# Residual rows added earlier in the last stage of a hybrid encoder, and a reordered start

## The chip, the cores and the metric

The kernel runs on one core of one Trainium2 chip. The metric is the device time of one execution in microseconds (us), taken as the median of several runs. One execution is also profiled, and the profile's span and instruction times come from that one.

## The reference, cut to what matters

One layer of a bidirectional encoder runs over two batches with shared weights: the prompt (512 rows of 1024) and the sample (1024 rows of 1024), all in fp32.

```python
def _trunk(x, ...):
    h = _rmsnorm(x, norm_attn_g)
    z = h @ w_in                                   # 1024 -> 1792: q, k, v, and the conv pair ca, cb
    a_out = _window_attn(q, k, v, bias, band, sink)  # window 128, T5 bias, a sink per head
    c = ca * sigmoid(cb)
    c = _dwconv(c, conv_dw_w, conv_dw_b)           # 31 taps
    c = silu(_layernorm(c, conv_ln_g, conv_ln_b))
    x = x + concat([a_out, c]) @ w_out
    h = _rmsnorm(x, norm_ffn_g)
    u = _dwconv(h @ w_up, ffn_dw_w, ffn_dw_b)      # 1024 -> 5632, 3 taps
    x = x + (silu(u[..., :D_FF]) * u[..., D_FF:]) @ w_down   # D_FF = 2816 -> 1024
    return _rmsnorm(x, norm_final_g)
```

Below, x1 is the value of x after the out-projection: the last residual sum adds it to the product with w_down.

## The kernel before, in words

**Products.** An fp32 operand is split into a high part, rounded to the fp32r format of TensorE, and a low part, the difference. A product is three matmuls: high by high, high by low, low by high (L1502, L1503, L1504; in the input projection all from L504). The high part is a cast on ScalarE, the low part a subtraction on VectorE or GpSimd (L1050 is the line of the helper `sub`, L1047 of the helper `add`). All matmuls that matter here are 128x128 by 128x512.

**Stages.** Input projection, attention and the 31-tap convolution, out-projection, the feed-forward part of the prompt, and last the up and the down product of the sample. These last two use a Strassen-Winograd scheme with 7 products in place of 8.

**The start.** A tile of weights in pieces (`w_first`, five DMAs from L214) and the eight blocks of the transposed prompt (`load_xT(0)`, L200) are loaded first. On ScalarE a tiny Exp (L220) draws in the table that the activations need. A few transposes of the identity (L224) run on TensorE meanwhile. For each weight piece in turn, `first_pieces` scales the x block (L459), casts the piece (L470) and takes its low half on GpSimd (L471); `beside` (L504) then issues six matmuls for each of the eight blocks. The sample's rows follow. They need the row scales, which come from the rows of x_prompt and end at L240.

**The down stage.** The products run in the order 1, 2, 5, 6, 7, 4, 3 (ORDER). Each is a sum over 11 pairs p (NPAIR) of blocks of the contracted axis. In a pair there are six row blocks tt with three matmuls each, so a product is 198 matmuls. The operands of pair p are loaded (`load_next`, from L1433 and L1440), summed or subtracted where the scheme wants it, and split (`operands`) four to six pairs ahead. A product fills three wide PSUM banks, two row blocks in each; there are four such banks, w in the profile. Two are taken at p = 0. The third, for tt = 4 and 5, is taken at p = HOLD, and the matmuls for the pairs before are then made up for. At the end of a product `evacuate` adds its banks to sums in SBUF, `u`, `e`, `o11` and `o12`, on VectorE; a bank is free for the next product after that. Product 3 has a loop of its own: z (tt 0, 1) from the start, zp (tt 4, 5) from p = HOLD, and at p = 4 two banks zs for the rest.

**The x1 rows.** `load_x1(t, n)` loads one quarter of x1 with six DMAs of 256 KB (L1514) into three tiles. `with_x(name, t, n)` adds it to one of the four sums: three adds of 128x1024, the first on VectorE and the other two on GpSimd.

**What sets the order.** Each engine works off its instructions in one order. In the last stages the order of TensorE and of the DMA issues on SyncE (SP) is that of the program. The order on ScalarE, VectorE and GpSimd is set when the kernel is built, by a scheduler that simulates the timeline.

Of the kernel before, what the change touches and what calls it, by code (L numbers as in the profile page):

```python
# [12 lines left out]
AF = mybir.ActivationFunctionType  # L13
ALU = mybir.AluOpType

P = 128
# [44 lines left out]
KL, WN = 16, 7  # L61
LN = 3
SUM_AT = (4, 6, 8, 10, 12, 14, 16, 18)
XP = (2, 4, 4, 8, 8, 10)
LZ = 6
AP = 1

# [37 lines left out]
def tile_hybrid_encoder(ctx: ExitStack, tc: tile.TileContext, xs, rel_bias, norm_attn_g, w_in,  # L105
                        attn_sink, conv_dw_w, conv_dw_b, conv_ln_g, conv_ln_b, w_out, norm_ffn_g,
                        w_up, ffn_dw_w, ffn_dw_b, w_down, norm_final_g, onehot, laid, outs):
    nc = tc.nc
# [8 lines left out]
    sb = Slots(lambda tag: sml if tag[0] == "s" else big,  # L117
               dict(q=(15, 4096), c=(4, 4352), h=(61, 2048), d=(2, 2304), s=(33, 64)))
# [12 lines left out]
    nhalf = cst.tile([P, 4], F32, name="nhalf")  # L131
    warm = cst.tile([P, 4], F32, name="warm")
# [63 lines left out]
    def load_xT(nt):  # L196
        n = 1 if nt == 0 else 2
        for k in range(0, KC, n):
            x = sb.tile([n, NT])
            nc.sync.dma_start(x[:], xT[nt][k:k + n].rearrange("k p t -> p k t"))  # L200
            for m in range(n):
                xq[nt, k + m] = (x, m)
            x = None

    def load_rows(nt):
        G, t0 = (GR[0], 0) if nt == 0 else (GR[1], 4 * (nt - 1))
        for tt in range(4):
            xq[nt, "row", tt] = load_x(G, t0 + tt)

    h1, xq, rbs, first_w = {}, {}, {}, []  # L210
    PIECES = ((0, 1), (1, 1), (2, 2), (4, 2), (6, 2))
    for k0, n in PIECES:
        w = sb.tile([n, 2 * P])
        nc.scalar.dma_start(w[:], laid["w_first"][k0:k0 + n].rearrange("k p c -> p k c"))  # L214
        first_w.append(w)
        w = None
    load_xT(0)
    load_rows(0)
    load_xT(1)
    nc.scalar.activation(warm[:], nhalf[:], AF.Exp)  # L220
    for _ in range(NW // 4):
        pt = bank("step")
        for i in range(4):
# [288 lines left out]
    cvw = cst.tile([P, 128], F32, name="cvw")  # L512
    fw = cst.tile([P, 192], F32, name="fw")
    nc.sync.dma_start(cvw[:, :CK * 4], laid["cvw"])
    load_xT(2)
    want_raw(2)
    nc.sync.dma_start(fw[:, :132], laid["fw"])
    nc.sync.dma_start(sinkb[:], attn_sink[0].partition_broadcast(P))
# [300 lines left out]
    def double_keys():  # L819
        for kv in range(NKV):  # L820
            for L in range(2):
                nc.gpsimd.tensor_copy(kt[1, kv][L][HD:P, :], kt[1, kv][L][0:HD, :].bitcast(F32))
                yield
# [69 lines left out]
    n, doubling = 0, double_keys()  # L893
# [152 lines left out]
    def add(out, a, b, eng=None):  # L1046
        (eng or nc.vector).tensor_tensor(out, a, b, op=ALU.add)  # L1047
# [176 lines left out]
    def wide():  # L1224
        return wide_banks.tile([W2])
# [7 lines left out]
    def armed(out, hi=None):  # L1233

        hi = hi or A[1, 0][0]
        nc.tensor.matmul(out, hi[:, 0:P], hi[:], start=True, stop=True)  # L1236
# [206 lines left out]
    ORDER = (1, 2, 5, 6, 7, 4, 3)  # L1443
# [48 lines left out]
    HOLD = 2  # L1492
# [16 lines left out]
    def load_x1(t, n):  # L1509
        xd[t, n] = pair2()  # L1510
        for w in range(3):
            for q in range(2):
                blk = 2 * t + q if w == 2 else 4 + 4 * t + 2 * w + q
                nc.sync.dma_start(xd[t, n][w][:, q * NT:(q + 1) * NT], x1d[blk][:, n * NT:(n + 1) * NT])  # L1514
# [26 lines left out]
    def with_x(name, t, n):  # L1541
        x = xd.pop((t, n))
        for w in range(3):
            add(acc[name][w][:], acc[name][w][:], x[w][:], nc.gpsimd if w else None)
# [55 lines left out]
    def down_step(k):  # L1600
        i, p = steps[k]
        if k > 1:
            next(rest, None)
        load_next(8 if k == 0 else 3 if len(pr) < CAP else 0)
        make(k + (LEAD + max(0, min(2, (k - 60) // 2)) if k else 1))
        if p == 0:
            pd.extend(wide() for _ in range(2))
        hold = 5 if i == ORDER[0] else HOLD
        if p == hold:
            pd.append(wide())  # L1610
        for tt in range(4):
            mm_down(pd[tt // 2][:, (tt % 2) * NT:(tt % 2 + 1) * NT], i, p, tt)
        hl[i, p] = None, hl[i, p][1]
        if p >= hold:
            for q in range(p + 1) if p == hold else (p,):
                for tt in (4, 5):
                    mm_down(pd[2][:, (tt % 2) * NT:(tt % 2 + 1) * NT], i, q, tt)
                hl.pop((i, q)), hp.pop((i, q))
        if i == 7 and p == 4:
            load_x1(0, 0)  # L1620
        if i == 7 and p == 8:
            with_x("o11", 0, 0)
        if i == 4 and p == XP[0]:
            load_x1(1, 1)
            fins.append(sb.tile([D]))
            nc.sync.dma_start(fins[0][:], norm_final_g.partition_broadcast(P))
            nc.scalar.activation(fins[0][:], fins[0][:], AF.Identity, scale=D ** 0.5)
        if i == 4 and p == XP[1]:
            with_x("e", 1, 1)
        if i == 4 and p == XP[2]:  # L1630
            load_x1(0, 1)
        if i == 4 and p == XP[3]:
            with_x("o12", 0, 1)
        if i == 4 and p == XP[4]:
            load_x1(1, 0)
        if i == 4 and p == XP[5]:
            with_x("u", 1, 0)
        if p == NPAIR - 1:
            evacuate(i, pd)
            while pd:  # L1640
                pd.pop(0)

    for j in range(2, NJ):
# [52 lines left out]
    for p in range(NPAIR):  # L1696
        load_next(LN)
        make(base + p + LZ)
        for tt in (0, 1):
            mm_down(z[:, tt * NT:(tt + 1) * NT], 3, p, tt)  # L1700
        if p == HOLD:
            zp = wide()
        if p >= HOLD:
            for q in range(p + 1) if p == HOLD else (p,):
                for tt in (4, 5):
                    mm_down(zp[:, (tt - 4) * NT:(tt - 3) * NT], 3, q, tt)
                hp.pop((3, q))
        if p == 4:
            for tt in (2, 3):
                zs.append(wide())  # L1710
                armed(zs[-1][:, L], hl[3, p][0][0])
                nc.scalar.copy(zs[-1][:, L], cut(o12, tt))
        if p in OTHER:
            blk = OTHER[p]
            tt = blk + 2 if blk < 4 else blk - 8
            finish(blk, (cut(u, tt), cut(e, tt)), False)
# [81 lines left out]
```

## Time and profile before

| | before |
|---|---|
| median of 3 runs | 1512.12 us (1510.12 to 1512.32) |
| the profiled execution | 1509.46 us |
| its span in the trace | 1507.7 us |
| granted TensorE clock, mean | 0.993 |
| last matmul begins | 1501.41 us |

A busy row of the profile gives each engine's busy time and its share of the span. A row of a timeline gives the start, the duration, the engine (a "q" behind it means that the engine issues a DMA), the line of the code, the operation with the tiles it writes and reads (buffer numbers left out), and in brackets the idle time before it with the instruction that ended it. Waits have the line that waited, what ended the wait, the total, the count and the longest. A row of windows gives, for one stretch of time, each engine's busy time with its count of instructions, then the granted TensorE clock (1.00 is full), the share of the DMA engines and their GB/s.

### The profile page before, as it was taken

To read this page: it belongs to the slowest core of one execution; us is meant where nothing else is said; L and a number is where in the kernel's file an instruction comes from. 1 tells how busy PE (TensorE), PEld (TensorE's weight loads), DVE (VectorE), ACT (ScalarE), POOL (GpSimd) and SP (SyncE) were. 2 spreads that over 40 slices of the span, in tenths; PEclk is the share of its full clock that TensorE was granted. 3 is DMA by queue.
4 is the path that set the end of the run, shared out by engine and by line. 5 is a ranking of instruction groups with operands and counts; after the bars stand their busy time and mean duration, and the time that the engine had idled before them with its cause. 6 is when DMAs were issued, how large, how long until landed. Compare 5 with 4: busy or idle time off the path is not lost. (4 is left out here: it accounts for less than half of the span.)

```text
span 1507.7 us, 19878 instructions
## 1 busy us (share of the span) xinstructions
PE 1478.4 (98%) x6736; PEld 1215.9 (81%) x6736; DVE 1115.0 (74%) x1512; ACT 801.8 (53%) x1421; POOL 779.7 (52%) x687
## 2 busy tenths in 40 slices
PE   8999999999999999999999999999999999999988
PEld 7888778777888888878788788888888888888776
DVE  7877945648999895566769888888886756657883
ACT  6424455567777876653464545454454453433354
POOL 3455253356987864332436666555654341214756
PEclk9999999999999999999999999999999999999999
DMA  9465241743433453763114334433323493446843
GB/s 377 154 173 143 89 112 36 243 145 129 154 122 127 144 170 130 226 208 105 70 59 137 133 133 133 133 126 126 130 102 111 163 339 124 132 151 208 270 134 153
DMA packets 124625, 228.19 MB, mean 151 GB/s; under 512 B 20419, under 2 KB 45763, under 8 KB 124396
## 3 DMA queue, kind: packets, MB, share of 16 engines
q1 hardware_dynamic: 122988, 225.32, 45.6%
q10 hardware_dynamic: 1536, 1.61, 0.3%
q8 instruction: 53, 0.87, 0.2%
q14 instruction: 48, 0.39, 0.1%
HBM read 166.83 MB, written 61.10 MB: 151 GB/s over the span
## 5 line engine op out<-in xcount | busy, mean ns | idle before, releaser
L159 POOL TENSOR_TENSOR q<-q,q 128x1024 fp32r<-128x1024 f32 x66 | 158.6, 2405 | 78.4 <-ACT q L158 47.1
L1050 POOL TENSOR_TENSOR q<-q,q 128x512 fp32r<-128x512 f32 x81 | 116.4, 1445 | 128.6 <-ACT q L1156 128.6
L1502 PE MATMUL w<-h,h 128*128 128x512 f32 x436 | 170.8, 392 | 5.7 <-DVE q L1047 5.7
L1050 DVE TENSOR_TENSOR h<-h,h 128x512 fp32r<-128x512 f32 (+1 forms) x153 | 127.0, 856 | 66.1 <-ACT h L1058 24.1
L1504 PE MATMUL w<-h,h 128*128 128x512 f32 x432 | 168.8, 391 | 0.0
L1503 PE MATMUL w<-h,h 128*128 128x512 f32 x426 | 166.7, 391 | 0.0
L293 PE MATMUL u<-h,q 128*128 128x512 f32 x384 | 151.0, 394 | 0.0
L295 PE MATMUL u<-h,q 128*128 128x512 f32 x384 | 150.4, 392 | 0.0
L294 PE MATMUL u<-h,q 128*128 128x512 f32 x384 | 150.1, 391 | 0.0
L1170 PE MATMUL w<-h,q 128*128 128x512 f32 x368 | 143.8, 391 | 0.9 <-ACT w L1261 0.6
L1172 PE MATMUL w<-h,q 128*128 128x512 f32 x368 | 143.7, 391 | 0.0
L1171 PE MATMUL w<-h,q 128*128 128x512 f32 x347 | 135.4, 390 | 0.0
L1050 POOL TENSOR_TENSOR h<-h,h 128x512 fp32r<-128x512 f32 (+1 forms) x38 | 56.3, 1484 | 148.6 <-ACT h L1485 112.9
L1058 ACT CAST h<-h 128x512 fp32r<-128x512 f32 x116 | 69.7, 620 | 104.2 <-DVE h L1050 38.4
L1502 PEld LDWEIGHTS w<-h,h 128*128 128x128 f32 x436 | 82.4, 189 | 23.7 <-DVE q L1047 6.5
L330 DVE SCALAR_TENSOR_TENSOR c<-d,cvw,c 128x512 f32<-128x512 f32 x128 | 95.9, 749 | 1.7
L158 ACT CAST q<-q 128x1024 fp32r<-128x1024 f32 x66 | 69.1, 1050 | 50.8 <-PE u L294 25.0
L1504 PEld LDWEIGHTS w<-h,h 128*128 128x128 f32 x432 | 81.7, 189 | 17.1
L1050 POOL TENSOR_TENSOR c<-q,c 128x512 fp32r<-128x512 f32 x46 | 73.1, 1598 | 40.6 <-ACT c L1156 40.5
L1503 PEld LDWEIGHTS w<-h,h 128*128 128x128 f32 x426 | 80.5, 189 | 16.8
L322 POOL TENSOR_TENSOR h<-h,h 128x512 f32<-128x512 f32 x62 | 80.5, 1301 | 18.5 <-ACT h L321 16.3
L295 PEld LDWEIGHTS u<-h,q 128*128 128x128 f32 x384 | 72.1, 188 | 14.7
(459 smaller groups left out, 4017.2 us busy)
## 6 DMA issues: line engine op xcount, KB each, us to landing
q<-in_laid_w_up SPq DMA_DIRECT2D x88, 512.0 KB, 4.0
ga<-q SPq DMA_DIRECT2D x65, 256.0 KB, 2.2
h<-gap SPq DMA_DIRECT2D x57, 256.0 KB, 3.6
h<-ga SPq DMA_DIRECT2D x57, 256.0 KB, 3.1
h<-in_w_down SPq DMA_DIRECT2D x52, 256.0 KB, 3.4
q<-in_laid_w_in SPq DMA_DIRECT2D x22, 512.0 KB, 4.0
gap<-h SPq DMA_DIRECT2D x44, 256.0 KB, 3.0
q<-in_x_sample SPq DMA_DIRECT2D x15, 512.0 KB, 7.2
```

Of the source, the lines that this page charges most:

```text
L159: (nc.vector if dve else nc.gpsimd).tensor_tensor(lo[:], raw[:], hi[:].bitcast(F32), op=ALU.subtract)
L293: nc.tensor.matmul(out, whi[:, kc, :], hi[:], start=(kc == 0), stop=False)
L294: nc.tensor.matmul(out, whi[:, kc, :], lo[:], start=False, stop=False)
L295: nc.tensor.matmul(out, wlo[:, kc, :], hi[:], start=False, stop=(kc == KC - 1))
L330: nc.vector.scalar_tensor_tensor(acc[:], src(t), w(t), acc[:], op0=ALU.mult, op1=ALU.add)
L1050: (eng or nc.vector).tensor_tensor(out, a, b, op=ALU.subtract)
L1170: nc.tensor.matmul(out, whi[:, s], hi[:], start=(start and c == 0), stop=False, **go)
L1171: nc.tensor.matmul(out, whi[:, s], lo[:], start=False, stop=False, **go)
L1172: nc.tensor.matmul(out, wlo[:, s], hi[:], start=False, stop=(stop and c == 3), **go)
L1502: nc.tensor.matmul(out, sh[:, c], th[:], start=(p == 0 and not seeded), stop=False, **go)
L1503: nc.tensor.matmul(out, sh[:, c], tl[:], start=False, stop=False, **go)
L1504: nc.tensor.matmul(out, sl[:, c], th[:], start=False, stop=(p == NPAIR - 1), **go)
```

## The change

**The start.** ScalarE's Exp now stands behind the load of `vecs` and ahead of its DMA issues. The first two weight pieces are issued on SP, one behind the first x block and one behind the second; the other three stay on ScalarE. `load_xT` becomes a generator so that the pieces can go in between.

**The down stage.** The quarter of x1 for o11 is loaded in product 6 at pair 3 and added at pair 7 (before: product 7, pairs 4 and 8). The quarter for o12 takes that place in product 7 (before: product 4, pairs 4 and 8). In product 4 the quarter for e moves from pairs 2 and 4 to 1 and 3, and that for u from pairs 8 and 10 to 3 and 6. The new HZ = 3 takes the place of HOLD = 2 in product 4 and for zp in product 3.

```diff
-XP = (2, 4, 4, 8, 8, 10)
+XP, HZ = (1, 3, 3, 6), 3
...
     PIECES = ((0, 1), (1, 1), (2, 2), (4, 2), (6, 2))
-    for k0, n in PIECES:
-        w = sb.tile([n, 2 * P])
-        nc.scalar.dma_start(w[:], laid["w_first"][k0:k0 + n].rearrange("k p c -> p k c"))
-        first_w.append(w)
-        w = None
-    load_xT(0)
+
+    def load_first(i, queue):
+        k0, n = PIECES[i]
+        first_w.append(sb.tile([n, 2 * P]))
+        queue.dma_start(first_w[i][:], laid["w_first"][k0:k0 + n].rearrange("k p c -> p k c"))
+
+    nc.scalar.activation(warm[:], nhalf[:], AF.Exp)
+    x_of_prompt = load_xT(0)
+    for i in range(2):
+        next(x_of_prompt)
+        load_first(i, nc.sync)
+    for i in range(2, len(PIECES)):
+        load_first(i, nc.scalar)
+    drawn(x_of_prompt)
     load_rows(0)
-    load_xT(1)
-    nc.scalar.activation(warm[:], nhalf[:], AF.Exp)
+    drawn(load_xT(1))
...
-        hold = 5 if i == ORDER[0] else HOLD
+        hold = 5 if i == ORDER[0] else HZ if i == 4 else HOLD
...
+        if i == 6 and p == 3:
+            load_x1(0, 0)
+        if i == 6 and p == 7:
+            with_x("o11", 0, 0)
         if i == 7 and p == 4:
-            load_x1(0, 0)
+            load_x1(0, 1)
         if i == 7 and p == 8:
-            with_x("o11", 0, 0)
+            with_x("o12", 0, 1)
...
         if i == 4 and p == XP[2]:
-            load_x1(0, 1)
+            load_x1(1, 0)
         if i == 4 and p == XP[3]:
-            with_x("o12", 0, 1)
-        if i == 4 and p == XP[4]:
-            load_x1(1, 0)
-        if i == 4 and p == XP[5]:
             with_x("u", 1, 0)
...
-        if p == HOLD:
+        if p == HZ:
             zp = wide()
-        if p >= HOLD:
-            for q in range(p + 1) if p == HOLD else (p,):
+        if p >= HZ:
+            for q in range(p + 1) if p == HZ else (p,):
```

Three places show how the instructions move. The lines of the changed kernel are up to 12 higher (L1047 becomes L1059, L1050 becomes L1062, L1502 becomes L1514).

ScalarE at the start of the program, before. The tiles h_1 to h_5 are the five weight pieces, h_6 and h_7 the first x blocks.

```order
L137 DMA vecs<-in_laid_vecs 128x72
L214 DMA h_1_90<-in_laid_w_first 128x256
L214 DMA h_2_92<-in_laid_w_first 128x256
L214 DMA h_3_94<-in_laid_w_first 128x2x256
L214 DMA h_4_96<-in_laid_w_first 128x2x256
L214 DMA h_5_98<-in_laid_w_first 128x2x256
L220 ACT_TABLE_LOAD
L220 ACTIVATE warm<-nhalf 128x4
L459 ACTIVATE h_24_165<-h_6_100,vecs 128x512
L470 CAST h_22_163<-h_1_90 128x256
L459 ACTIVATE h_28_179<-h_7_102,vecs 128x512
L470 CAST h_26_177<-h_2_92 128x256
```

The same place in the changed kernel. Here h_2 and h_4 are the first two pieces (loaded from SP), h_5 to h_7 the other three, h_1 and h_3 the first x blocks.

```order
L137 DMA vecs<-in_laid_vecs 128x72
L223 ACT_TABLE_LOAD
L223 ACTIVATE warm<-nhalf 128x4
L221 DMA h_5_99<-in_laid_w_first 128x2x256
L221 DMA h_6_101<-in_laid_w_first 128x2x256
L221 DMA h_7_103<-in_laid_w_first 128x2x256
L471 ACTIVATE h_24_165<-h_1_91,vecs 128x512
L482 CAST h_22_163<-h_2_93 128x256
L482 CAST h_30_191<-h_5_99 128x512
L471 ACTIVATE h_28_179<-h_3_95,vecs 128x512
L482 CAST h_36_215<-h_6_101 128x512
L482 CAST h_26_177<-h_4_97 128x256
```

The table load stands ahead of the issues, and two issues have left the engine. The casts of the third and the fourth piece (h_5, h_6) now stand ahead of the cast of the second (h_4). GpSimd takes the low halves in the same new order.

VectorE at the end of product 4, before: from the x1 add of u (q_1747) to the add of the product's first bank (w_60) to it. The rows between are the low halves of product 3's operands.

```order
L1047 TENSOR_TENSOR q_1747_11425<-q_1747_11425,q_2193_13345 128x1024
L1050 TENSOR_TENSOR h_2202_13365<-h_2146_13148,h_2201_13364 128x512
L1050 TENSOR_TENSOR q_2218_13442<-h_2173_13265,q_2218_13442 128x512
L1050 TENSOR_TENSOR h_2204_13369<-h_2157_13195,h_2203_13368 128x512
L1050 TENSOR_TENSOR h_2206_13373<-h_2158_13197,h_2205_13372 128x512
L1050 TENSOR_TENSOR q_2217_13439<-h_2172_13263,q_2217_13439 128x512
L1050 TENSOR_TENSOR h_2213_13405<-h_2163_13226,h_2212_13404 128x512
L1050 TENSOR_TENSOR h_2215_13409<-h_2164_13228,h_2214_13408 128x512
L1047 TENSOR_TENSOR q_1747_11425<-w_60_13008,q_1747_11425 128x1024
```

The changed kernel, the last rows up to the add of the same bank.

```order
L1062 TENSOR_TENSOR h_2198_13362<-h_2151_13170,h_2197_13361 128x512
L1062 TENSOR_TENSOR h_2200_13366<-h_2152_13172,h_2199_13365 128x512
L1062 TENSOR_TENSOR h_2204_13374<-h_2161_13209,h_2203_13373 128x512
L1062 TENSOR_TENSOR h_2211_13406<-h_2166_13238,h_2210_13405 128x512
L1062 TENSOR_TENSOR h_2213_13410<-h_2167_13240,h_2212_13409 128x512
L1062 TENSOR_TENSOR h_2216_13438<-h_2175_13278,h_2215_13437 128x512
L1062 TENSOR_TENSOR h_2218_13442<-h_2176_13280,h_2217_13441 128x512
L1059 TENSOR_TENSOR q_1747_11425<-w_60_13020,q_1747_11425 128x1024
```

The x1 add of u has left this stretch: 19 splits stand between it and the bank's add instead of 7, the first of them still of product 4. On GpSimd five splits now follow its two x1 adds of u before the first row of the final norm, where three did.

TensorE in product 3 where zp begins, before. The bank w_63 is z, w_64 is zp.

```order
L1502 MATMUL w_63_13438<-h_2189_13316,h_2187_13312 128x512
L1503 MATMUL w_63_13438<-h_2190_13317,h_2187_13312 128x512
L1504 MATMUL w_63_13438<-h_2189_13316,h_2188_13313 128x512
L1502 MATMUL w_64_13500<-h_2176_13272,h_2178_13276 128x512
L1503 MATMUL w_64_13500<-h_2177_13273,h_2178_13276 128x512
```

The changed kernel at the same place.

```order
L1514 MATMUL w_63_13436<-h_2199_13365,h_2197_13361 128x512
L1515 MATMUL w_63_13436<-h_2200_13366,h_2197_13361 128x512
L1516 MATMUL w_63_13436<-h_2199_13365,h_2198_13362 128x512
L1514 MATMUL w_64_13514<-q_2179_13287,h_2180_13290 128x512
L1515 MATMUL w_64_13514<-q_2179_13287,h_2180_13290 128x512
```

Before, 18 matmuls into z stand ahead of the first into zp. Now there are 24; the six more are those of pair 3.

More of the change, by code (lines that the diff above doesn't have):

```diff
@@ L203, in load_xT @@
             x = None
+            yield
     def load_rows(nt):
@@ L208, in load_rows, with drawn @@
             xq[nt, "row", tt] = load_x(G, t0 + tt)
+    def drawn(items):
+        for _ in items:
+            pass
     h1, xq, rbs, first_w = {}, {}, {}, []
     PIECES = ((0, 1), (1, 1), (2, 2), (4, 2), (6, 2))
-    for k0, n in PIECES:
-        w = sb.tile([n, 2 * P])
-        nc.scalar.dma_start(w[:], laid["w_first"][k0:k0 + n].rearrange("k p c -> p k c"))
-        first_w.append(w)
-        w = None
-    load_xT(0)
+    def load_first(i, queue):
[10 more added lines that the diff above has]
+    drawn(x_of_prompt)
     load_rows(0)
-    load_xT(1)
-    nc.scalar.activation(warm[:], nhalf[:], AF.Exp)
+    drawn(load_xT(1))
     for _ in range(NW // 4):
@@ L514, in tile_hybrid_encoder @@
     nc.sync.dma_start(cvw[:, :CK * 4], laid["cvw"])
-    load_xT(2)
+    drawn(load_xT(2))
     want_raw(2)
```

## The prediction

> **What bounds the kernel now.** I read the head of the page first, then the waits of TensorE, then the timeline around its longest ones.
>
> ```profile
> span 1507.7 us, 19878 instructions
> PE 1478.4 (98%) x6736; PEld 1215.9 (81%) x6736; DVE 1115.0 (74%) x1512; ACT 801.8 (53%) x1421; POOL 779.7 (52%) x687
> ```
>
> TensorE is busy for 98% of the span. The change removes no matmul, so it can only win TensorE's idle time, and time in which TensorE runs at a reduced clock. The waits (line, what ended the wait, total, count, longest) are few:
>
> ```profile
> PE w L1502 <- DVE q L1047: 5.7, 2, 4.7
> PE u L504 <- ACT h L470: 2.6, 1, 2.6
> ```
>
> The first row is the down stage: twice TensorE stood until VectorE had added a bank of a finished product to its sum (L1047). The second is the start of the program. Both edits of the change aim at these rows. The timeline of TensorE at the longer one, and then the engines over it (PE, PEld, DVE, ACT, POOL busy with counts, granted clock, DMA share, GB/s):
>
> ```profile
> 1452.24 0.39 PE L1504 MATMUL w<-h,h 128*128 128x512 f32 x1
> 1452.92 0.39 PE L1504 MATMUL w<-h,h 128*128 128x512 f32 x1
> 1457.98 0.79 PE L1502 MATMUL w<-h,h 128*128 128x512 f32 x1 [4.67 <-DVE q L1047]
> 1463.10 0.40 PE L1502 MATMUL w<-h,h 128*128 128x512 f32 x1
> 1446.40:1454.70 8.30, 6.91 (x31) 5.39 (x29) 8.16 (x5) 4.33 (x9) 8.28 (x4) 1.00 0.34 127
> 1458.00:1463.10 5.10, 5.10 (x13) 3.99 (x14) 5.10 (x7) 2.71 (x6) 1.55 (x2) 0.52 0.00 0
> ```
>
> Three matmuls take 1452.92 - 1452.24 = 0.68 us, so the pace is 0.227 us. The next one should have begun at 1453.15 and began at 1457.98: 4.83 us are lost in standing. After it the granted clock is 0.52, and the twelve matmuls up to 1463.10 take 5.12 us instead of 12 x 0.227 = 2.72: another 2.40. The place costs **7.23 us**. It is the first matmul of product 3 into its third bank (zp), which product 4 must have given back. Why VectorE was late:
>
> ```profile
> 1446.55 2.83 DVE L1050 TENSOR_TENSOR q<-h,q 128x512 fp32r<-128x512 f32 x1
> 1449.30 4.62 DVE L1050 TENSOR_TENSOR h<-h,h 128x512 fp32r<-128x512 f32 x2
> 1453.84 1.74 DVE L1050 TENSOR_TENSOR q<-h,q 128x512 fp32r<-128x512 f32 x1
> 1455.51 1.28 DVE L1050 TENSOR_TENSOR h<-h,h 128x512 fp32r<-128x512 f32 x2
> 1456.71 1.21 DVE L1047 TENSOR_TENSOR q<-w,q 128x1024 f32<-128x1024 f32 x1
> 1446.42 2.40 POOL L1047 TENSOR_TENSOR q<-q,q 128x1024 f32<-128x1024 f32 x1 [2.81 <-DMA q<-x1d]
> 1448.79 2.88 POOL L1047 TENSOR_TENSOR q<-q,c 128x1024 f32<-128x1024 f32 x1
> ```
>
> Six splits stand ahead of the bank's add on VectorE. Alone such a split takes 0.64 us (the pair in 1.28); here the six take 1456.71 - 1446.55 = 10.16, against 3.84. They are long exactly while POOL works (busy 8.28 of the 8.30 us of the first window): its two late adds of x1, 2.40 and 2.88, begun after a wait of 2.81 for their x1 load, and then its own splits. So the late x1 rows make VectorE late, and VectorE the bank.
>
> **The change part by part. Product 3's zp at pair 3 instead of 2.** Six more matmuls go ahead of the wait: 6 x 0.227 = 1.36 us of slack. The z operands of pair 3 must then be ready 1.36 us sooner; their splits stand ahead of the bank's add in either order, so they are. Product 4 asks for its own third bank a pair later too, where no wait stood: 0.
>
> **x1 rows sooner.** Product 4 holds two sets of x1 adds instead of three, and the last set comes at pair 6 instead of 10, four pairs of 18 x 0.227 = 4.09 us each sooner. This takes three things out of the way of the bank's add. One add of 128x1024 leaves VectorE: 1.21 (the row at 1456.71, same shape) to 3.49:
>
> ```profile
> 1412.84 3.49 DVE L1047 TENSOR_TENSOR q<-q,q 128x1024 f32<-128x1024 f32 x1 [2.21 <-DMA q<-x1d]
> ```
>
> Two POOL adds of 5.28 us together come out of the last six splits. The six lost 10.16 - 3.84 = 6.3 us beside a POOL that was never idle; by share the adds account for 5.28/8.30 of it, 4.0 us. With the 1.36 from zp that is 1.36 + 1.21 + 4.0 = 6.6 us against a lateness of 4.83: the stall goes, with 1.8 us over, and with it the reduced clock. I take **-7.2**. The other end: the adds meet other splits of the same VectorE queue sooner and only the 1.36 and the 1.21 count. [...]
>
> [...]
>
> **The shorter stall** (1.03 us, start of product 4) has this chain:
>
> ```profile
> 1398.22 2.87 POOL L1050 TENSOR_TENSOR h<-h,h 128x512 fp32r<-128x512 f32 x2 [9.41 <-DMA h<-ga]
> 1401.13 0.69 DVE L1050 TENSOR_TENSOR h<-h,h 128x512 fp32r<-128x512 f32 x1 [2.44 <-POOL h L1050]
> 1405.41 0.50 PE L1502 MATMUL w<-h,h 128*128 128x512 f32 x1 [1.03 <-DVE q L1047]
> ```
>
> A load ends POOL's wait, POOL's split ends VectorE's, and the add follows. Loads and the order of these steps stay. In product 7 the x1 adds of o12 take the place of those of o11, in POOL's idle 9.41 us (2.40 + 2.88). I keep this stall: 0, with -1.2 (it goes) and +1.2 (it doubles) as ends.
>
> **Product 6** now holds x1 adds and six more issues on SP, ahead of its weight loads. The nearest row is the set that product 7 issues:
>
> ```profile
> 1369.94 3.54 SPq L1514 DMA_DIRECT2D c<-x1d  x6
> 1335.58 4.86 DVE L1050 TENSOR_TENSOR h<-h,h 128x512 f32<-128x512 f32 x7 [1.84 <-DMA h<-in_w_down]
> ```
>
> The last operand differences of product 6 are done at 1340.4. The stall at 1405.41 lies six matmuls into product 4, which so began at 1405.41 - 1.18 - 1.36 = 1402.9; a product is 198 x 0.227 = 44.9 us, so product 6 ended near 1357.9 and its last pair began near 1353.8: 13.4 us cover 3.54 of issues and a POOL add. Price 0; without that cover, 3.5.
>
> **The start.** ScalarE before, then TensorE and POOL there:
>
> ```profile
> 1.16 1.42 ACTq L214 DMA_DIRECT2D h<-in_laid_w_first  x3
> 1.16 4.06 ACTq L214 DMA_DIRECT2D h<-in_laid_w_first  x5
> 5.25 1.28 ACT L220 ACT_TABLE_LOAD   x1 [5.25 <-DMA h<-in_laid_w_first]
> 6.66 0.71 ACT L459 ACTIVATE h<-h,vecs 128x512 fp32r<-128x512 f32 x1
> 7.27 0.39 ACT L470 CAST h<-h 128x256 fp32r<-128x256 f32 x1
> 9.11 0.60 ACT L470 CAST h<-h 128x512 fp32r<-128x512 f32 x1
> 7.71 0.50 PE L504 MATMUL u<-h,h 128*128 128x512 f32 x1 [2.55 <-ACT h L470]
> 12.32 0.40 PE L504 MATMUL u<-h,h 128*128 128x512 f32 x1
> 7.74 7.25 POOL L471 TENSOR_TENSOR h<-h,h 128x256 fp32r<-128x256 f32 x5 [5.98 <-ACT h L470]
> 7.74 2.15 POOL L471 TENSOR_TENSOR h<-h,h 128x256 fp32r<-128x256 f32 x2 [5.98 <-ACT h L470]
> h<-in_laid_w_first ACTq DMA_DIRECT2D x3, 256.0 KB, 5.6
> h<-in_laid_xpT SPq DMA_DIRECT2D x1, 256.0 KB, 3.0
> 21.40 1.28 ACT L240 ACTIVATE h<-ident,s 128x128 f32<-128x128 f32 x4 [1.90 <-POOL s L143]
> ```
>
> The table load (1.28) and the warm-up now come before three issues instead of after five. From 1.16: 1.28 + 0.12 + three issues of 4.06/5 = 0.81 end at 5.0; the activation and the cast need 0.61 + 0.39, so the first matmul comes near 6.0 instead of 7.71. But the new ACT order puts the casts of pieces 2 and 3 ahead of the second activation and the cast of piece 1, and POOL follows with its low halves in the order 0, 2, 3, 1, 4. Pieces 2 and 3 are issued at 2.6 and 3.4 and took 5.6 us to land before: 8.2 and 9.0. Then ACT does cast 2 to 8.8, the activation to 9.4, cast 3 to 10.0, cast 1 to 10.4; a wide POOL split is (7.25 - 2.15)/3 = 1.70, so POOL has 2 at 10.5, 3 at 12.2 and 1 at 13.3. The last two matmuls of the second block wait for it, and the third block begins near 13.9 instead of 12.32: +1.6, and +1.8 with issues of 1 us. The other end: issues at the pace of the first three (1.42/3 = 0.47) and pieces that land in the 3.0 us of the first x piece. The first matmul then comes at 5.0, POOL has piece 0 at 6.1, 2 at 7.8, 3 at 9.5 and 1 at 10.6, and the third block begins near 11.1, a gain of 1.2. More than 1.0 can't be kept: the sample rows hang on the row scales (21.40, after a wait for POOL) and these on loads that are not issued sooner. The ends are **-1.0 and +1.8**; I take **0**: two weight pieces fewer queue on ACT, which speaks for a landing between the two, and a landing of 4.3 us gives +0.1 by the same steps.
>
> [...]
>
> The sum: 0 + 0 + 0 - 7.2 on the profiled execution's 1509.46 gives 1502.3. The median of the runs lies 1512.12 - 1509.46 = 2.66 higher, and I carry that over: **1505.0**.
>
> **The rivals.**
>
> [...]
> - *It doesn't do what it says.* VectorE is late because of its whole backlog, 74% busy over the span, not because of the x1 adds; the bank's add stays behind the same last splits. Only the 1.36 counts, of which a start at +1.3 takes all: **1512**.
> - *Slower: SP's queue holds the loads.* In product 4 the second set of x1 loads follows the first by two pairs, on SP ahead of the last weight loads; its tiles must have been given back by VectorE and POOL, and whatever waits there holds every later load, while VectorE waits for it at its x1 add with product 4's last splits behind. These were done early enough:
>
> ```profile
> 1433.91 1.28 DVE L1050 TENSOR_TENSOR h<-h,h 128x512 fp32r<-128x512 f32 x2
> 1420.87 2.37 SPq L1514 DMA_DIRECT2D q<-x1d  x4
> c<-x1d SPq DMA_DIRECT2D x14, 256.0 KB, 5.8
> ```
>
>   They end at 1435.2; the last pair begins 36 matmuls before the zp matmul that was due at 1453.15, at 1445.0. Nine splits of 0.64 and the add of 1.21 must come between, so it decides when the loads land after 1438.0. A lateness of 10 us beyond this costs 10 + 2.4 of clock: 1505.0 + 12.4 = **1517.4**. Against it: the loads of pair 4 were issued at 1420.87, those of pair 3 come a pair sooner, at 1416.8, the last of six some 3.3 later, and land in 5.8: 1425.9, 12 us of cover.
> [...]
>
> **How the numbers follow.** Forecast 0.62, exclusion moves 0.14, nothing gained 0.09, SP's queue 0.07, clock rule 0.08. A measurement of this kernel tells some 0.2%, 3.0 us, from no change. Forecast and clock rule are faster, the exclusion case lies on the bound and is halved: faster 0.62 + 0.08 + 0.07 = 0.77; same 0.09 + 0.07 = 0.16; slower 0.07. The forecast's own range is 1505.0 - 1.0 - 1.2 - 1 for the spread of the runs = 1501.8, up to 1505.0 + 1.8 = 1506.8. The range goes to 1510.0 to hold the exclusion case, and leaves out the other two, 0.16.
>
> **What would show it.** Down stage right: no wait of TensorE above 1 us at product 3's first zp matmul, a granted clock near 1.0 there, and the bank's add on VectorE beginning less than 4.2 us after product 4's last matmul (24 matmuls last 5.4, the add 1.2). [...] Start right: first matmul between 5.0 and 6.0, third block between 11.1 and 13.9, and the first sample-row matmul moved by less than 1 us against 20.49:
>
> ```profile
> 20.49 1.98 PE L504 MATMUL a<-h,h 128*128 128x512 f32 x8
> ```
>
> Wrong altogether: a new wait of TensorE in products 6, 7 or 4 on a split whose load or x1 add was late.

## The result

| | median | runs | ratio to before (95% interval) |
|---|---|---|---|
| before, beside the change | 1512.22 us | 4, 1510.12 to 1512.87 | |
| the change | 1502.80 us | 4, 1501.59 to 1504.36 | 0.995 (0.9932 to 0.9968) |
| before, in a later series | 1508.90 us | 9, 1506.82 to 1510.77 | |
| the change, in that series | 1501.86 us | 5, 1499.46 to 1502.58 | 0.9947 (0.9934 to 0.9961) |

The change is about 0.5% faster, 7 to 9 us. The ratios are estimates of their own and not the quotients of the medians, which would be 0.9938 and 0.9953; the gains of the experiments below go by their ratios. The forecast was 1505.0 with a range of 1501.8 to 1510.0. The profiled execution of the change took 1504.36 us with a span of 1502.6 us, 5.1 us below that of before.

The programs have the same 6736 matmuls. Set against each other one by one, counted in order, their starts tell where the 5.1 us of the two profiled executions lie:

| matmul | before | after | after - before |
|---|---|---|---|
| first of the projection | 7.71 | 5.24 | -2.47 |
| first of the third block | 12.32 | 10.58 | -1.74 |
| first of a sample row | 20.49 | 19.03 | -1.46 |
| sixth of product 4 (last before its wait) | 1404.00 | 1403.53 | -0.47 |
| first of product 3 | 1449.07 | 1451.20 | +2.13 |
| last of the program | 1501.41 | 1496.31 | -5.10 |

From the first matmul of product 3 to the end the gain is 7.23 us. Product 4 gives 2.60 us back, and of the 2.47 us at the start 0.47 are left when product 4 begins.

### The profile page after: what moved, and what is told of

Read it like the earlier page. It is cut to its first block, busy times and chain, and to the rows that moved or that the text cites. A ratio compares the mean times of both kernels' runs of the same rounds, so it can differ in the third digit from the quotient of the medians.

```text
span 1502.6 us, 19890 instructions
## 1 busy us (share of the span) xinstructions
PE 1475.6 (98%) x6736; PEld 1213.3 (81%) x6736; DVE 1108.8 (74%) x1512; ACT 802.9 (53%) x1421; POOL 775.7 (52%) x687
## 3 DMA queue, kind: packets, MB, share of 16 engines
q10 hardware_dynamic: 1248, 1.35, 0.3%
## 5 line engine op out<-in xcount | busy, mean ns | idle before, releaser
L1062 POOL TENSOR_TENSOR q<-q,q 128x512 fp32r<-128x512 f32 x81 | 116.6, 1447 | 128.0 <-ACT q L1168 128.0
L1062 DVE TENSOR_TENSOR h<-h,h 128x512 fp32r<-128x512 f32 (+1 forms) x152 | 128.3, 871 | 64.7 <-ACT h L1070 25.6
L1514 PE MATMUL w<-h,h 128*128 128x512 f32 x436 | 170.5, 391 | 2.0 <-DVE q L1059 2.0
L1062 POOL TENSOR_TENSOR h<-h,h 128x512 fp32r<-128x512 f32 (+1 forms) x39 | 54.6, 1401 | 144.1 <-ACT h L1497 113.0
L1514 PEld LDWEIGHTS w<-h,h 128*128 128x128 f32 x436 | 82.1, 188 | 19.5 <-DVE q L1059 2.4
L1062 POOL TENSOR_TENSOR c<-q,c 128x512 fp32r<-128x512 f32 x46 | 73.1, 1599 | 40.1 <-ACT c L1168 40.0
```

The costliest lines, as they stand in the source:

```text
L1062: (eng or nc.vector).tensor_tensor(out, a, b, op=ALU.subtract)
L1514: nc.tensor.matmul(out, sh[:, c], th[:], start=(p == 0 and not seeded), stop=False, **go)
```

## The profile after

The waits of TensorE in the changed kernel, the longest ones:

```profile
PE w L1514 <- DVE q L1059: 2.0, 1, 2.0
PE a L696 <- ACT h L684: 1.7, 2, 1.4
PE u L516 <- ACT h L482: 1.7, 2, 1.3
```

The wait of 4.7 us at the third bank of product 3 is gone; of two waits on the down stage's banks one is left. VectorE at that place, then the two x1 adds of GpSimd, then the first zp matmul on TensorE:

```profile
1436.81 3.70 DVE L1062 TENSOR_TENSOR h<-h,h 128x512 fp32r<-128x512 f32 x4
1442.87 1.47 DVE L1062 TENSOR_TENSOR h<-h,h 128x512 fp32r<-128x512 f32 x2 [2.36 <-ACT h L1070]
1445.55 4.92 DVE L1062 TENSOR_TENSOR h<-h,h 128x512 fp32r<-128x512 f32 x6 [1.21 <-ACT h L1070]
1451.08 0.69 DVE L1062 TENSOR_TENSOR h<-h,h 128x512 fp32r<-128x512 f32 x1 [0.61 <-ACT h L1070]
1451.68 1.22 DVE L1059 TENSOR_TENSOR q<-w,q 128x1024 f32<-128x1024 f32 x1
1428.37 2.74 POOL L1059 TENSOR_TENSOR q<-q,q 128x1024 f32<-128x1024 f32 x1 [1.20 <-DMA q<-x1d]
1431.07 2.86 POOL L1059 TENSOR_TENSOR q<-q,c 128x1024 f32<-128x1024 f32 x1
1456.64 0.39 PE L1514 MATMUL w<-q,h 128*128 128x512 f32 x1
```

The x1 adds now end at 1433.9, 18 us ahead of the bank's add. The last splits take 4.92 us for six instead of 10.16, and VectorE stands between them, waiting for casts of ScalarE (2.36, 1.21, 0.61). The bank's add ends at 1452.90, the zp matmul comes at 1456.64: 3.7 us of slack where 4.83 were missing. Of this turn of some 8.5 us, VectorE brings 5.03 (the bank's add begins at 1451.68 instead of 1456.71), the six matmuls 1.36, and 2.13 come from TensorE itself, which reached product 3 that much later. The same 8 us of both kernels, before first (PE, PEld, DVE, ACT, POOL, granted clock, DMA share, GB/s):

```profile
1444.00:1452.00 8.00, 8.00 (x37) 6.61 (x36) 7.44 (x5) 5.05 (x10) 5.58 (x3) 1.00 0.59 206
```

```profile
1444.00:1452.00 8.00, 8.00 (x37) 6.64 (x36) 6.15 (x9) 5.43 (x11) 1.71 (x2) 1.00 0.44 148
```

VectorE gets nine instructions through in 6.15 us where it got five through in 7.44, and GpSimd's busy time fell from 5.58 to 1.71 us.

The wait that is left, at the start of product 4, in TensorE's timeline, and then the window behind it:

```profile
1403.53 0.39 PE L1516 MATMUL w<-h,h 128*128 128x512 f32 x1
1405.91 0.50 PE L1514 MATMUL w<-h,h 128*128 128x512 f32 x1 [2.00 <-DVE q L1059]
1407.40 0.63 PE L1514 MATMUL w<-h,h 128*128 128x512 f32 x1
```

```profile
1407.40:1410.80 3.40, 3.40 (x9) 2.63 (x8) 3.40 (x5) 1.21 (x2) 3.40 (x2) 0.50 0.98 327
```

It grew from 1.03 to 2.00 us. TensorE came 0.47 us sooner and the bank 0.50 us later. Behind it the clock was halved for 3.4 us, which cost another 1.6 us.

The start of the changed kernel: ScalarE, TensorE, and ScalarE's first activation of a sample row.

```profile
1.16 1.28 ACT L223 ACT_TABLE_LOAD   x1 [1.16 <-PEq L1790]
1.23 1.44 ACTq L221 DMA_DIRECT2D h<-in_laid_w_first  x3
3.77 0.72 ACT L471 ACTIVATE h<-h,vecs 128x512 fp32r<-128x512 f32 x1 [1.10 <-DMA vecs<-in_laid_vecs]
4.78 1.00 ACT L482 CAST h<-h 128x256 fp32r<-128x256 f32 x2 [0.29 <-DMA h<-in_laid_w_first]
5.24 0.50 PE L516 MATMUL u<-h,h 128*128 128x512 f32 x1 [0.33 <-ACT h L482]
8.25 0.50 PE L516 MATMUL u<-h,h 128*128 128x512 f32 x1 [1.34 <-ACT h L482]
10.00 0.50 PE L516 MATMUL u<-h,h 128*128 128x512 f32 x1 [0.56 <-POOL h L483]
19.03 2.44 PE L516 MATMUL a<-h,h 128*128 128x512 f32 x8
18.26 1.34 ACT L471 ACTIVATE h<-q,vecs 128x512 fp32r<-128x512 f32 x2 [1.37 <-DMA q<-in_laid_xsT]
```

The table load and the three issues run side by side. From 2.7 us on ScalarE waits for data. The first matmul is 2.47 us sooner, the second block waits for the cast of piece 1 (1.34), its last two matmuls for GpSimd's low half of that piece (0.56). The sample's rows then start when their x block has landed, at 18.26. In the kernel before that was the same moment:

```profile
18.17 1.34 ACT L459 ACTIVATE h<-q,vecs 128x512 fp32r<-128x512 f32 x2 [1.35 <-DMA q<-in_laid_xsT]
```

There TensorE was still busy with the prompt until 20.49 and didn't notice. So what the start gains is cut by a transfer that comes no sooner.

## The experiments

The theory: the last x1 adds on GpSimd stretch VectorE's splits, so the bank of product 4 is added late, TensorE stands, and its clock falls. The expectations call this stretching exclusion: in before a split took 0.64 us beside an idle GpSimd and 2.83 beside one of its x1 adds. The rivals: VectorE's backlog or SP's late loads make the bank late and the x1 adds only happen to stand there; the extra slack of HZ = 3 is what counts; the start brings a part. Four kernels take the change apart.

**The start alone** (e1_start): the diff of the start, nothing of the down stage.

```diff
-    for k0, n in PIECES:
-        ...
-    load_xT(0)
+    nc.scalar.activation(warm[:], nhalf[:], AF.Exp)
+    ...
+    drawn(x_of_prompt)
```

> The start edit alone on the kernel before. In the profiles of before and after, the first matmul came 2.47 us sooner, but at the 67th matmul (20 us) only 1.0 us was left. Theory (the start is worth what the row scales allow): first matmul near 5.2, no reduced clock window in the first 16 us, third block near 10.6, and 1.0 us less at 20 us; the whole run 1.0 us below before, 1511.2, and the wait of 4.7 us ahead of product 3's zp stays. Rival (the start accounts for the part of the 9.4 us that the down stage's 7.2 does not): 2.2 us or more below before, 1510 or less.

Measured: 1509.17 us over 12 runs against 1509.14 over 23, ratio 0.9997 (0.9987 to 1.0007). The row of waits shows that the one at zp stayed:

```profile
PE w L1514 <- DVE q L1059: 6.2, 2, 5.7
```

Its first matmul came 2.70 us sooner than before, its 67th, at 20.3 us, 0.62. So the start is worth what is left after the sample's x blocks, half a microsecond in the trace and nothing that the runs can tell (at most 2 us by the interval). The rival is out; the expected 1.0 lies inside the interval.

**The down stage alone** (e2_down): XP, HZ and the moved loads and adds, with the old start.

```diff
-XP = (2, 4, 4, 8, 8, 10)
+XP, HZ = (1, 3, 3, 6), 3
...
+        if i == 6 and p == 3:
+            load_x1(0, 0)
```

> The down-stage edit alone (x1 rows sooner and third bank at pair 3) on the kernel before. Theory: the wait at zp and the clock behind it go, 7.2 us, so 1505.0; the wait at the start of product 4 stays between 1 and 2 us. Rival (the down stage gains more than the stall, since the waits in products 6 and 7 get less too): 8.4 us or more below before, 1503.8 or less.

Measured: 1502.56 us over 5 runs, ratio 0.9951 (0.9939 to 0.9963), so 7.4 us. The whole gain is here. It is nearer to the theory's 7.2 than to the rival's 8.4, which the interval (5.6 to 9.2 us) does not exclude. Its waits have none at zp; at the start of product 4 there is 0.6 us, less than the 1 to 2 that I expected:

```profile
PE w L1502 <- DVE q L1047: 0.6, 1, 0.6
```

**Only the third bank later** (e3_hz).

```diff
-        hold = 5 if i == ORDER[0] else HOLD
+        hold = 5 if i == ORDER[0] else HZ if i == 4 else HOLD
...
-        if p == HOLD:
+        if p == HZ:
             zp = wide()
```

> Only the third bank at pair 3 in products 4 and 3 (HZ = 3), with the x1 rows where they were before. Theory (VectorE is late because POOL's late x1 adds stretch its last splits): only 1.36 us of the 4.83 us of standing go, 3.5 us stay, and the clock still falls behind it: about 1510.8, a gain of 1 to 2. Rival (the extra 1.36 us and the new order are what mattered): the wait is under 1 us and the run 6 us or more below before, 1506 or less.

Measured: 1504.25 us over 12 runs, ratio 0.9969 (0.9957 to 0.9981): 4.7 us, and a wide spread (1501.85 to 1509.47). The expectation of 1 to 2 us was wrong. The zp matmul waited 0.44 us, in TensorE's timeline:

```profile
1456.37 0.50 PE L1503 MATMUL w<-h,h 128*128 128x512 f32 x1 [0.44 <-DVE q L1048]
```

I had taken the x1 rows as fixed in time since their place in the program is. They were not. The issue of u's x1 block on SP, GpSimd's first add of it and the bank's add on VectorE in the timeline of e3_hz, and then SP in that of before:

```profile
1435.39 1.81 SPq L1515 DMA_DIRECT2D q<-x1d  x4
1442.71 2.76 POOL L1048 TENSOR_TENSOR q<-q,q 128x1024 f32<-128x1024 f32 x1
1455.10 1.21 DVE L1048 TENSOR_TENSOR q<-w,q 128x1024 f32<-128x1024 f32 x1
```

```profile
1438.94 0.32 SPq L1440 DMA_DIRECT2D h<-ga  x1
1439.35 1.81 SPq L1514 DMA_DIRECT2D q<-x1d  x4
```

With the bank a pair later the loads left SP 4.0 us sooner and GpSimd's add began 3.7 us sooner (1446.42 before); the bank's add came 1.6 us sooner, and 1.36 us of slack were added. The rest came from TensorE, which in this execution reached product 3 at 1450.32, 1.25 us later than in before. Had it been on time, 4.83 - 1.6 - 1.36 = 1.9 us of standing would be left by this estimate; that fits the wide spread of the runs, but no run shows it. In before, SP issued nothing from 1433.8 to 1438.94 and x1 stood behind that load. By SP's waits the load stood 5.1 us there until a split of VectorE had ended, at 1438.92; in e3_hz its wait for VectorE was 0.5. Why VectorE gives that load its tile sooner with HZ = 3 stays open. So HZ = 3 works in part by the slack and in part by x1 rows that come sooner on their own.

**Only the x1 rows** (e4_x): as the change, with HZ = 2 and the old start.

```diff
-XP, HZ = (1, 3, 3, 6), 3
+XP, HZ = (1, 3, 3, 6), 2
```

> Only the x1 rows sooner, with the third bank at pair 2 as before (HZ = 2). Theory (the x1 adds are the cause): VectorE saves 1.2 us for the add that leaves product 4 and about 4 us of exclusion, against a lateness of 4.83, so the wait at zp is under 1 us, the clock stays up, and the run is near 1505.5. Rival (the exclusion only moves along with the adds): 2 to 4 us of wait stay and the run is at 1508 or above.

Measured: 1503.38 us over 5 runs, ratio 0.9958 (0.9946 to 0.997): 6.3 us. No wait at zp; VectorE's timeline:

```profile
1445.50 4.92 DVE L1050 TENSOR_TENSOR h<-h,h 128x512 fp32r<-128x512 f32 x6 [1.21 <-ACT h L1058]
1451.64 1.22 DVE L1047 TENSOR_TENSOR q<-w,q 128x1024 f32<-128x1024 f32 x1
```

The bank's add ended at 1452.86 and the zp matmul was due at 1453.05. The x1 rows alone just suffice, with 0.2 us; HZ = 3 adds its 1.36 as a reserve. The rival, that the stretching moves along with the adds and the wait stays, failed here: earlier in the product there is room for it. Two splits beside the x1 adds took 5.71 us there (from 1429.48), and VectorE still stood 3.05 us for a cast ahead of 1441.55.

Two kernels then ask directly whether the x1 adds are the cause, and whether by stretching VectorE's splits.

**No x1 adds to u** (e5_no_add), on the kernel before. This quarter of the output lacks its residual.

```diff
         if i == 4 and p == XP[5]:
-            with_x("u", 1, 0)
+            xd.pop((1, 0))
```

> The kernel before without the three adds of the last x1 quarter to u; its loads stay (left out: this quarter of the sample's output lacks its residual). Theory (the late x1 adds, through POOL's exclusion of VectorE, make the bank's add late): no POOL add between 1440 and 1452, VectorE's last splits at 0.6 to 0.8 us each, the wait ahead of product 3's zp under 1 us, the granted clock up there, span near 1500.5. Rival (SP's late loads of product 3's operands or the backlog make it late, the adds only happen to stand there): the wait stays above 2.5 us, span above 1505.

Measured, one run: 1503.02 us, span 1501.2. The wait at zp was gone, and the 37 matmuls of the window from 1444 to 1452 ran at a granted clock of 1.00. VectorE's timeline up to the add of the bank:

```profile
1446.14 0.68 DVE L1050 TENSOR_TENSOR h<-h,h 128x512 fp32r<-128x512 f32 x1
1446.79 0.70 DVE L1050 TENSOR_TENSOR q<-h,q 128x512 fp32r<-128x512 f32 x1
1452.01 1.21 DVE L1047 TENSOR_TENSOR q<-w,q 128x1024 f32<-128x1024 f32 x1
```

The loads stayed: SP issued the first of them at 1440.01, at 1439.35 in before. The three splits just ahead of the bank's add took 3.74 us together, more than the 0.6 to 0.8 each that I expected; splits of GpSimd ran beside them. Even so the add began 4.70 us sooner than in before, of which the x1 add that VectorE itself was spared is 1.2. The late adds are the cause; backlog and SP's loads alone don't make the bank late.

**All x1 adds to u on VectorE** (e6_dve), on the kernel before.

```diff
-            add(acc[name][w][:], acc[name][w][:], x[w][:], nc.gpsimd if w else None)
+            add(acc[name][w][:], acc[name][w][:], x[w][:], nc.gpsimd if w and name != "u" else None)
```

> The kernel before with all three x1 adds to u on VectorE (before: one there, two on POOL), nothing left out. VectorE gets 2 x 1.21 us more work, POOL 5.28 less. Theory (exclusion): the last six splits take some 4 us instead of 10.2, so the bank's add comes 10.2 - 4 - 2.4 = 3.8 us sooner; of the 4.83 us of standing about 1 stays, and the run is 4 to 6 us below before. Rival (backlog): VectorE is 2.4 us later, the wait is about 7 us and the run 2 us or more above before.

Measured: 1507.93 us over 10 runs, ratio 0.999 (0.9979 to 1.0), so 0 to 3 us below before. The wait shrank from 4.7 to 3.7, neither theory's number. The row of waits, and then VectorE's splits and GpSimd's in the timeline:

```profile
PE w L1502 <- DVE q L1047: 4.4, 2, 3.7
```

```profile
1448.35 0.69 DVE L1050 TENSOR_TENSOR h<-h,h 128x512 fp32r<-128x512 f32 x1
1451.30 1.79 DVE L1050 TENSOR_TENSOR q<-h,q 128x512 fp32r<-128x512 f32 x1
1453.01 2.96 DVE L1050 TENSOR_TENSOR h<-h,h 128x512 fp32r<-128x512 f32 x3
1450.22 2.32 POOL L1050 TENSOR_TENSOR d<-h,h 128x512 fp32r<-128x512 f32 x1 [4.96 <-ACT h L1485]
```

The first three splits here take 0.69 each beside an idle GpSimd. A later one takes 1.79 and three others 2.96 together while GpSimd does its own splits (1450.22 to 1454.2). In before, the seven splits from the end of the x1 add to the bank's add took 1456.71 - 1445.72 = 10.99 us; here, from 1448.35 to the bank's add at 1455.89 and less an x1 add of 1.14 between, the seven take 6.40. So the two x1 adds on GpSimd had cost VectorE 4.6 us, and GpSimd's own splits cost it another 1.9 (6.40 against 7 x 0.64). The adds now cost VectorE about 2.4 itself, and VectorE came to them 1.3 us later in this execution (1445.86 against 1444.58): 4.6 - 2.4 - 1.3 = 0.9 us, the 1 us measured. My expectation had overlooked GpSimd's splits. So VectorE's splits did take longer beside GpSimd's work, but what makes the bank late is x1 work that arrives at the end, on whichever of the two engines it is done.

The last kernels go after what the change still pays.

**Product 4's second bank at pair 1** (e7_bank), on the changed kernel; six more matmuls stand ahead of the wait.

```diff
-            pd.extend(wide() for _ in range(2))
+            pd.extend(wide() for _ in range(1 if i == 4 else 2))
...
+        if i == 4 and p == 1:
+            pd.append(wide())
```

> The changed kernel with product 4's second bank taken at pair 1 instead of pair 0: six more matmuls (1.36 us) stand ahead of the first that needs product 7's bank, and 6 later ones make it up. Theory (the wait at the start of product 4 hangs on a chain that the change did not touch): the 2.0 us shrink to 0.6, no window of reduced clock behind it, and the run is 1.4 to 3 us below the changed kernel, 1500 to 1501.5 where that is at 1502.8. Rival (the chain moves along, since the operand tiles are given back later): the wait stays at 1.5 us or more and the run within 1 us of the changed kernel.

Measured: 1501.25 us over 6 runs (1497.6 to 1503.5), ratio 0.9939 (0.9923 to 0.9956). The wait shrank as expected (TensorE's timeline), and the next three matmuls came 0.23 us apart (1408.34, 1408.57, 1408.81):

```profile
1408.01 0.50 PE L1514 MATMUL w<-h,h 128*128 128x512 f32 x1 [0.43 <-DVE q L1059]
```

Against the change's 0.995 and 0.9947 this is about 1 us less, with intervals that overlap, so the expected gain of 1.4 to 3 us is not shown.

**That bank with the old start, beside the change itself** (e10_bank_old_start, e9_after), in one series.

> The changed kernel again, beside the next one on the same chip, as the base for it: 1502.8 by its first runs, so 1501.5 to 1504 with 0.995 of before. No theory differs on it.

> The start of the kernel before, the down stage of the changed one, and product 4's second bank at pair 1. Theory (the wait at the start of product 4 is what the changed kernel still pays, 1.4 to 2 us and at times a window of reduced clock, 1.7; the start edit is worth nothing in the runs): 1.5 to 3 us below the changed kernel of the same call, about 1500.5. Rival (the gain of the bank is inside the noise, or the start edit's 1 us counts): within 1 us of the changed kernel.

Measured: the change 1501.86 us, 0.9947 (0.9934 to 0.9961); the bank with the old start 1503.27 us, 0.9958 (0.9945 to 0.9971). The expected gain of 1.5 to 3 us is not there; the median lies 1.4 us above the change, with intervals that overlap, which is nearer to the rival. Two reasons show in the traces. The wait at the start of product 4 is not always 2.0 us: in the second profile of the change it was 1.5 and the granted clock stayed at 1.00 from 1405.6 to 1411, in e2_down, with the old start, 0.6, in e4_x 0.1. And slow stretches lie elsewhere in some executions and not in others: e10's trace has them near 158, 339 and 359 us, e9's in that part only near 159; the mean granted clocks were 0.993 and 0.996. I can't name a version that beats the change beyond doubt; e7_bank has the lowest median, and whether it or the start edit is worth its 1 us stays open.

**The sample's x ahead of the prompt's rows** (e8_xs), on the changed kernel.

```diff
-    load_rows(0)
     drawn(load_xT(1))
+    load_rows(0)
```

> The changed kernel with the sample's first x blocks issued ahead of the prompt's rows. Theory (what the start edit gains is lost again because the sample's x blocks, behind 2 MB of prompt rows, land at 18 us): the first sample-row matmul comes at 18.7 instead of 19.03 or sooner, but the row scales come some 4 us later, at 23 to 24 us instead of 19.7, and the step that needs them stands; 0 to 2 us above the changed kernel. Rival (the row scales are not needed that soon): 1 us or more below the changed kernel.

Measured: 1504.85 us over 10 runs, ratio 0.9968 (0.9958 to 0.9977), 2 to 3 us above the change. The expectation of 0 to 2 us was too low. The x block landed 4.6 us sooner (the activation at 13.63 instead of 18.26). TensorE could not use it: the first sample-row matmul came at 20.58, since the second block's wait was 1.75 us here and a slow stretch followed it (9.74 to 13.16). The prompt's row scales came late, in the timeline:

```profile
25.64 1.28 ACT L252 ACTIVATE h<-ident,s 128x128 f32<-128x128 f32 x4 [0.28 <-POOL s L143]
```

```profile
PE a L255 <- ACT h L252: 1.7, 1, 1.7
```

These scales went from 19.71 to 25.64. But the wait in the second row, from TensorE's waits, is not theirs: it ended at 50.15, at the scales of the sample's first rows, and a slow stretch from 50.70 to 57.53 followed (mean granted clock of the execution 0.994, of the change's 0.997). Counted matmul by matmul, e8_xs was 1.0 us behind the change at 40 us and 7.0 behind it after this stretch. So the step that I expected to stand did not stand; a later one did, and what made its scales late I did not trace. The DMA engines are full in this part of the program, as this window of the changed kernel shows (share 1.06), so putting one load ahead may hold the others back.

```profile
5.20:12.00 6.80, 4.87 (x19) 3.36 (x20) 3.45 (x4) 6.03 (x11) 5.65 (x5) 1.00 1.06 397
```

The order of the change is the better one.

## Why the prediction was right, and where it was off

**The 7.2 us at product 3's zp.** Right in mechanism and size, and with its sign: the bank's add began 0.7 us after product 4's last matmul (1450.97), where less than 4.2 was asked. Measured from the first matmul of product 3 to the end of the program: 7.23 us in the first pair of profiles, and 7.24 in the second profile of the change (1449.42 and 1494.52 against 1449.07 and 1501.41). By the runs the down stage is worth 7.4 us (e2_down).

**What takes the lateness away.** Forecast: 1.36 + 1.21 + 4.0, with 1.8 us over. The 4.0, taken by share of GpSimd's busy time, measured 4.6 in e6_dve. VectorE's part of the sum is 1.21 + 4.0 = 5.2, and the bank's add came 5.03 us sooner in the changed kernel and 5.07 in e4_x. The trace after has 3.7 us over, but 2.13 of them are TensorE's own delay in product 4; without it 1.6 are over against the 1.8 forecast. VectorE now waits for ScalarE's casts between its splits. I had not named these casts as the next bound.

**Product 3's bank at pair 3.** Costed at 1.36 us of slack. Alone it brought 4.7 us by the runs; in its trace it also let the x1 loads go 4 us sooner, and TensorE came 1.25 us later. The changed kernel shows the same dependence the other way: I had its last x1 loads issued at 1416.8, and they left SP at 1421.37, behind a load that waited 8.8 us for a split of GpSimd. I had read x1's time as set by its place in the program; it hangs on the queue it stands in.

**The shorter stall**, taken as 0 with ends of -1.2 and +1.2. It was +2.60 in the first profile, outside: the standing grew by 0.97, inside the bound, and I left the clock out of it, 1.63 us. In other executions it was smaller (0.6 in e2_down, 0.1 in e4_x). The spread comes from TensorE's side. The first matmul into the bank began at 1405.91 in the first profile of the change, 1405.76 in the second and 1405.74 in e2_down, while the matmul ahead of it began at 1403.53, 1403.84 and 1404.73: in these three the bank comes at the same time, and a TensorE that arrives early waits. So what TensorE gains ahead of product 4, by the start for instance, can be lost here. The traces also show where the bank's 0.50 us arise, though no run tests it alone: the chain waits for two splits of GpSimd, which took 3.32 us instead of 2.87 beside a split that VectorE now does there (1399.42, 1.02 us). In e4_x that split is not there, the two took 2.86, and the bank's matmul began at 1405.29.

**Product 6**, costed at nothing behind 13.4 us of cover: no wait of TensorE there in any of these traces.

**The start**, taken as 0 within -1.0 and +1.8: the runs say 0.9997 (0.9987 to 1.0007), so the number was right. The working was not; it had two faults, and both make the gain too small. I put the three issues behind the table load on ScalarE and so pieces at 8.2 and 9.0 us; they run beside it, all three issued by 2.7, and the third block began at 10.58, below my 11.1 to 13.9. And the cap was put on the row scales; it is the sample's x block that lands at 18.2 in both kernels. The first sample-row matmul moved by 1.46, more than the 1 us I allowed. The number held because the gain was lost again behind it, in the first profile of the change to 1.0 us at 24 us and to 0.47 at product 4. I had not worked that out, so it was luck.

**The carry of 2.66 us** from the profiled execution to the median is the term that moved the forecast most: without it the sum is 1502.3 against 1502.8 and 1501.86 measured. It came from three runs of before. Later series of the same kernel have medians of 1509.14, 1509.34 and 1508.90 (23, 22 and 9 runs), within 0.6 us of the profiled 1509.46. So the range held with little to spare: 1501.86 lies 0.06 us above its lower end. Nor did the uncarried sum hit for the right reason alone: in the profiled pair the change took 1504.36, 2.1 us above 1502.3, which is product 4's 2.60 less the 0.47 of the start.

**The rivals.** The case called exclusion moves (0.14, and the range's 1510.0), in which the adds only stretch other splits and the 1.36 and the 1.21 alone count, is shown by no run: in e4_x the wait at zp was gone and the gain was 6.3 us. That nothing is gained failed on e2_down; that SP's queue holds the loads, only in its size: they left 4.6 us later than I had them and VectorE's x1 add waited 1.71 us for one, but GpSimd's second add had its tile at 1431.07, ahead of the 1438.0 at which it would have counted. The clock rule (0.08), a start whose gaps leave the clock alone, is not shown as a rule by any run: with gaps of 1.34 and 0.56 the matmuls of the first profile ran at a granted clock of 1.00 up to 12 us, and the 1.9 us that the slow pace costs in before were gone (twelve matmuls in 12.32 - 7.71 = 4.61 us instead of 2.72, at a granted clock of 0.63). That brought little, because the sample's rows wait for their load; in e9_after a gap of 1.78 was followed by 3.4 us at 0.50.

## What to carry to other kernels

An add that only has to be done some time before the end should be done as soon as its operand can be there, not in the last stretch where the engine that frees a bank is needed; moving it to another engine there helped little (e6_dve, 0.999). When the place of a load in a queue is unchanged, its time need not be (4.0 us in e3_hz): look at what stands ahead of it in the queue. Before counting a gain at a program's start, look for the next transfer that it does not move.

## What the runs showed of the hardware

- Waits of TensorE were followed by a halved clock in some places and not in others. One of 2.00 us was followed by 3.4 us at a granted clock of 0.50, beginning 1.5 us after the wait ended (1407.40). Waits of 1.03 (before), 1.41 (e3_hz) and 1.5 (e9_after) at the same place were followed by a clock of 1.00. In the wait of 4.67 us of before the clock fell at 1456.06, and it stayed at 0.50 for 6.8 us. At the start, a gap of 1.78 was followed by it (e9_after, timeline and window) and one of 1.34 (the first profile of the change) not:

```profile
8.50 0.58 PE L516 MATMUL u<-h,h 128*128 128x512 f32 x1 [1.78 <-ACT h L482]
```

```profile
8.80:12.20 3.40, 3.40 (x9) 2.23 (x8) 2.57 (x2) 3.40 (x7) 3.08 (x3) 0.50 1.06 411
```

The slow matmuls came 0.43 us apart instead of 0.227 (the change, 1407.40 to 1410.81), so one such stretch in a dense stream cost some 1.6 us.
- The length of a wait did not decide alone. In before, a wait of 1.34 us that ended at 159.25 and waits of 0.57 and 0.58 us that ended at 642.26 and 643.46 were each followed by 3.4 us at half clock:

```profile
159.25 0.77 PE L293 MATMUL b<-h,q 128*128 128x512 f32 x1 [1.34 <-DVE h L442]
642.26 0.63 PE L733 MATMUL a<-ident,h 128*128 128x128 f32 x4 [0.57 <-issue]
643.46 0.63 PE L684 MATMUL a<-h,h 128*128 128x512 f32 x1 [0.58 <-DVE h L694]
158.95:162.40 3.45, 3.15 (x8) 2.50 (x9) 3.37 (x8) 0.92 (x3) 0.18 (x1) 0.51 0.38 148
643.68:647.10 3.42, 3.42 (x9) 2.40 (x9) 3.12 (x7) 1.14 (x2) 1.83 (x3) 0.50 1.07 382
```

In the change a wait of 1.35 us that ended at 158.07 was followed by it too (0.50 from 158.1 to 161.5), the one of 1.34 at the start was not, and from 640 to 648 the clock was 1.00. No run moved a wait on purpose, so what else decides is not shown.
- DMA issues on ScalarE's queue went on while it loaded its table: 1.23 to 2.67 beside 1.16 to 2.44 in the change. The other way round the load waited: in the kernel before it began at 5.25, when the fifth issue (1.16 to 5.22) ended.
- A 128x512 subtraction on VectorE took 0.69 us beside an idle GpSimd (e6_dve, 1448.35) and up to 2.90 beside its x1 add (before, 1429.95).
